# Encoder layer on one core: the split activations and the weight tiles moved to multiples of 2 KB in the SBUF partition

## The chip, the cores and the metric

The kernel runs on one core of one Trainium2 chip. The metric is device time in microseconds, from one launch; lower is better. The matrix engine is called TensorE or PE, its weight loads PEld, the vector engine VectorE or DVE, the scalar engine ScalarE or ACT, the general engine GpSimd or POOL, the engine that issues most DMAs SyncE or SP. SBUF is the on-chip memory with 128 partitions; an address below is a byte offset in a partition, the same for all 128.

## The reference

One encoder layer over 256 positions of width 2048, in float32:

```python
h = rmsnorm(x, norm1_gain)
proj = h @ w_in                       # 2048 x 6144: q, k, v of both head groups
# 4 differential heads: (softmax1 - lam * softmax2) V; 8 dilated-window heads, 3 patterns each
x = x + concat([o_d, o_l]) @ w_out    # 2048 x 2048
h2 = rmsnorm(x, norm2_gain)
g, u = split(h2 @ w_gate_up)          # 2048 x 11264
g = depthwise_conv(g, conv_w, conv_b) # width 3 over positions
x = x + (silu(g) * u) @ w_down        # 5632 x 2048
return rmsnorm(x, final_gain)
```

## The kernel before

Nearly all of the work is in four large matrix products. To keep float32 accuracy on a faster format, every operand is split in two float32r parts, hi (the rounded value) and lo (the remainder), by `split` (L118): ACT copies the value into hi (L121, or L124 with a gain), DVE subtracts hi from the value and writes lo (L122, or L125). A product is then three matmuls that add in PSUM: hi by hi, hi by lo, lo by hi.

The weights come as 196 tiles of 1 MB (`raw`, L80, three buffers). Each is used as two units of 1024 columns; `split_unit` (L198) makes `whi` and `wlo` of a unit (L200 and L201, four buffers each), three units ahead of the matmuls. `products` (L212) issues a unit's matmuls by `mm` (L209), so all of them carry line L210. There are two forms, and every matmul is preceded by a load of its stationary operand:

- Form A, 12 matmuls to a unit: a 128x128 block of the activations is stationary (512 bytes in a partition), 512 columns of weights are moving (2048 bytes). The stages are v (32 units, activations `hT`), o (32 units, `mT`) and d (88 units, `aT`).
- Form B, 24 matmuls to a unit: a 128x128 block of weights is stationary, 256 columns of activations are moving (1024 bytes). The stages are qk (64 units, `hT`) and gate/up (176 units, `h2T`, which has the memory of `hT`).

The stages run in the order v, qk, o, gate/up, d. Post-processing (attention scores, transposes, evacuations) is hung on slots after the units; in qk and o it puts short bursts of other matmuls between units, in gate/up and d none after the first few units.

SBUF is given out by pools. The pool `keep` (L53) comes first, then `stg` (L54: raw, whi, wlo), then `att` (L59) or, after attention, `mlp`. In a pool, tags lie one after the other in the order in which the program first asks for them, each rounded up to 32 bytes. `hT` is asked for at L128, after `sm`, `tl`, `ident`, `ones` and `mhalf`:

```python
mhalf = keep.tile([128, 2], F32, name="mhalf")                 # L115
hT = keep.tile([128, KT, 2, S], F32R, name="hT", tag="hT")     # L128
hi = stg.tile([128, 1024], F32R, name="whi", tag="whi")        # L200
```

What follows in `keep` sets where `stg` begins, and so where everything later begins. The functions that the change touches:

Of the kernel before, what the change touches and what calls it, by code (L numbers as in the profile page):

```python
# [9 lines left out]
F32 = mybir.dt.float32  # L10
F32R = mybir.dt.float32r
# [5 lines left out]
S = 256  # L17
D = 2048
KT = D // 128
# [30 lines left out]
def encoder_layer(ctx, tc, xT_d, x_d, w_d, sm_d, tab_d, fg_d, id_d, oh_d, lnc_d, out_d):  # L50
    nc = tc.nc
    PSUM = bass.MemoryType.PSUM
    keep = ctx.enter_context(tc.tile_pool(name="keep", bufs=1))  # L53
# [13 lines left out]
    nc.vector.memset(warm, 0.0)  # L67
    sm = keep.tile([128, N_SM], F32, name="sm")
    nc.gpsimd.dma_start(sm, sm_d)
    xT = att.tile([128, KT, S], F32, name="xT", tag="mT", bufs=1)  # L70
    tl = keep.tile([128, 1], F32, name="tl")
    nc.scalar.activation(tl, warm[:, :1], AF.Copy)
# [39 lines left out]

    ones = keep.tile([128, 128], F32, name="ones")
    nc.gpsimd.memset(ones, 1.0)
    mhalf = keep.tile([128, 2], F32, name="mhalf")  # L115
    nc.gpsimd.memset(mhalf, -0.5)

    def split(hi, lo, src, gain=None):  # L118
# [6 lines left out]
            nc.vector.scalar_tensor_tensor(lo, src, gain, hi.bitcast(F32),  # L125
                                           op0=ALU.mult, op1=ALU.subtract)

    hT = keep.tile([128, KT, 2, S], F32R, name="hT", tag="hT")  # L128

    def split_x(kt):  # L130
        split(hT[:, kt, 0], hT[:, kt, 1], xT[:, kt], sm[:, C_G1 + kt:C_G1 + kt + 1])
# [649 lines left out]
```

## Time and profile before

| what | value |
|---|---|
| median of 3 runs | 1146.08 us (1145.84 to 1146.66) |
| time of the profiled execution | 1146.24 us |
| its span, first to last instruction | 1144.5 us |
| PE busy | 1132.1 us, 99% of the span |
| PEld busy | 1054.2 us, 92% |
| DVE busy | 677.3 us, 59% |
| ACT busy | 548.4 us, 48% |
| mean granted TensorE clock | 0.995 |

The profiled execution spends 1.7 us outside its span. A matmul's duration in the trace reaches past the start of the next one, since matmuls are pipelined. What a matmul costs is therefore its pitch: the time from its start to the next one's start, read as the length of a piece of the chain divided by the matmuls in it.

### The profile page before, as it was taken

The numbers are of one execution on the slowest core, as the hardware profiler recorded it, in microseconds if no ns is written. First come the engines' busy times: TensorE is split into PE (matmuls) and PEld (weight loads), VectorE is DVE, ScalarE is ACT, GpSimd is POOL, SyncE is SP. The second block draws the span as 40 slices with busy tenths as digits, with TensorE's granted clock in tenths as the row PEclk, the third lists the DMA queues.
The fourth block names the chain that finished last, engine by engine and source line by source line (L and its number), as shares of the span: only waits on it lengthen the run. The fifth ranks groups of instructions, "written<-read, shape, count | busy, mean of one in ns | idle before, by whom it ended". The sixth has DMA issues, their size and how long they took to land.

```text
span 1144.5 us, 18680 instructions
## 1 busy us (share of the span) xinstructions
PE 1132.1 (99%) x7924; PEld 1054.2 (92%) x7924; DVE 677.3 (59%) x841; ACT 548.4 (48%) x770; POOL 21.9 (2%) x40
## 2 busy tenths in 40 slices
PE   8999999999999999999999999999999999999996
PEld 6879999999988899999999999999999888888885
DVE  6845667756656576666666566656565545454543
ACT  7544456565555554444444454445444434343432
POOL 0000000010000000000000000000000000000000
PEclk9999999999999999999999999999999999999998
DMA  9578545454444555555454545454555655555552
GB/s 330 194 258 319 181 169 183 165 195 165 172 157 163 205 184 185 185 184 194 175 201 171 212 155 219 163 207 160 209 183 186 221 192 206 190 187 194 205 186 74
DMA packets 34092, 219.87 MB, mean 192 GB/s; under 512 B 3904, under 2 KB 4288, under 8 KB 9432
## 3 DMA queue, kind: packets, MB, share of 16 engines
q1 hardware_dynamic: 31536, 211.17, 51.5%
q0 software_dynamic: 1776, 6.69, 1.6%
q8 instruction: 62, 1.02, 0.3%
q10 hardware_dynamic: 696, 0.81, 0.2%
q14 instruction: 22, 0.18, 0.0%
HBM read 216.54 MB, written 5.27 MB: 194 GB/s over the span
## 4 chain that ended last, share of the span: by engine, by line
PE 98%; DMA 0%; issue 0%; ACT 0%; DVE 0%; POOLq 0%; POOL 0%; DVEq 0%
PE acc L210 90%; PE at L210 7%; PE at L387 0%; DMA sm<-sm 0%; PE at L518 0%; PE at L452 0%; ACT jk L630 0%; POOLq L777 0%; PE at L248 0%; POOL r L636 0%; PE at L150 0%; DVEq L777 0%; ACT hT L124 0%; DVE x L642 0%; DVE x L628 0%
## 5 line engine op out<-in xcount | busy, mean ns | idle before, releaser
L122 DVE TENSOR_TENSOR wlo<-raw,whi 128x1024 fp32r<-128x1024 f32 (+1 forms) x400 | 475.4, 1201 | 283.3 <-ACT whi L121 283.2
L121 ACT ACTIVATE whi<-raw 128x1024 fp32r<-128x1024 f32 (+1 forms) x400 | 408.9, 1036 | 287.6 <-PE acc L210 213.5
L210 PE MATMUL acc<-h2T,whi 128*128 128x256 f32 x2816 | 360.7, 281 | 0.0
L210 PEld LDWEIGHTS acc<-h2T,whi 128*128 128x128 f32 x2816 | 344.1, 189 | 0.1
L210 PE MATMUL acc<-h2T,wlo 128*128 128x256 f32 x1408 | 194.5, 281 | 0.0
L210 PEld LDWEIGHTS acc<-h2T,wlo 128*128 128x128 f32 x1408 | 178.7, 189 | 0.0
L210 PE MATMUL acc<-whi,aT 128*128 128x512 f32 x528 | 162.8, 389 | 0.0
L210 PE MATMUL acc<-hT,whi 128*128 128x256 f32 x1024 | 128.6, 278 | 0.0
L210 PEld LDWEIGHTS acc<-hT,whi 128*128 128x128 f32 x1024 | 121.7, 188 | 0.1
L210 PEld LDWEIGHTS acc<-whi,aT 128*128 128x128 f32 x528 | 99.1, 188 | 20.7
L210 PE MATMUL acc<-wlo,aT 128*128 128x512 f32 x264 | 102.7, 389 | 0.0
L210 PE MATMUL acc<-whi,hT 128*128 128x512 f32 x256 | 82.1, 399 | 2.0 <-ACT hT L124 2.0
L210 PE MATMUL acc<-whi,mT 128*128 128x512 f32 x256 | 82.7, 395 | 0.0
L210 PE MATMUL acc<-hT,wlo 128*128 128x256 f32 x512 | 68.7, 276 | 0.0
L210 PEld LDWEIGHTS acc<-hT,wlo 128*128 128x128 f32 x512 | 62.9, 188 | 0.0
L210 PEld LDWEIGHTS acc<-whi,hT 128*128 128x128 f32 x256 | 48.8, 191 | 14.3 <-ACT hT L124 2.7
L572 ACT ACTIVATE y<-gs,sm 128x256 f32<-128x256 f32 x44 | 24.1, 595 | 75.3 <-DVE gs L564 75.3
L210 PEld LDWEIGHTS acc<-wlo,aT 128*128 128x128 f32 x264 | 49.5, 188 | 10.1
L210 PEld LDWEIGHTS acc<-whi,mT 128*128 128x128 f32 x256 | 48.1, 188 | 9.7
L210 PE MATMUL at<-whi,aT 128*128 128x512 f32 x176 | 54.4, 389 | 0.0
L210 PE MATMUL acc<-wlo,hT 128*128 128x512 f32 x128 | 50.7, 396 | 0.0
L210 PE MATMUL acc<-wlo,mT 128*128 128x512 f32 x128 | 49.9, 390 | 0.0
(120 smaller groups left out, 617.3 us busy)
## 6 DMA issues: line engine op xcount, KB each, us to landing
raw<-w SPq DMA_DIRECT2D x191, 1024.0 KB, 4.9
raw<-w SPq DMA_DIRECT2D x8, 512.0 KB, 7.6
Z<-Td POOLq DMA_DIRECT2D x1, 3072.0 KB, 20.6
Xb<-Z POOLq DMA_DIRECT2D x12, 192.0 KB, 3.2
x<-x SPq DMA_DIRECT2D x4, 512.0 KB, 12.4
xT<-xT SPq DMA_DIRECT2D x7, 256.0 KB, 6.9
raw<-w SPq DMA_DIRECT2D x4, 256.0 KB, 5.3
fg<-fg POOLq DMA_DIRECT2D x1, 1024.0 KB, 5.0
```

The lines of the kernel that those rows point to most:

```text
L121: nc.scalar.activation(hi, src, AF.Copy)
L122: nc.vector.tensor_sub(lo, src, hi.bitcast(F32))
L210: nc.tensor.matmul(out, lhsT, rhs, start=start, stop=stop)
L572: nc.scalar.activation(y[:, c], gs[:, 1:S + 1], AF.Identity, bias=sm[:, C_CB + f:C_CB + f + 1], scale=w[1])
```

## The change

Two edits. `hT` is asked for right after `sm`, ahead of `tl`, `ident`, `ones` and `mhalf`. And the tile of `mhalf` has 34 columns instead of 2, of which the first two are used as before; the other 128 bytes are filling.

```diff
     sm = keep.tile([128, N_SM], F32, name="sm")
     nc.gpsimd.dma_start(sm, sm_d)
+
+    hT = keep.tile([128, KT, 2, S], F32R, name="hT", tag="hT")
     xT = att.tile([128, KT, S], F32, name="xT", tag="mT", bufs=1)
...
-    mhalf = keep.tile([128, 2], F32, name="mhalf")
+    mhalf = keep.tile([128, 34], F32, name="mhalf")[:, :2]
     nc.gpsimd.memset(mhalf, -0.5)
...
-    hT = keep.tile([128, KT, 2, S], F32R, name="hT", tag="hT")
```

On every engine the instructions stand in the same order with the same operands, shapes and waits; only addresses differ. The places that the declarations give, in bytes from a partition's start and as the remainder by 2048 (the whole hi or lo of one row block of activations is 1024 bytes, one buffer of `whi` or `wlo` 4096 bytes, so all blocks and buffers of a tile share the remainders below, up to multiples of 512):

| tile | before | remainder | after | remainder |
|---|---|---|---|---|
| hT, h2T | 19520 | 1088 | 18432 | 0 |
| ident | 18464 | 32 | 51232 | 32 |
| ones | 18976 | 544 | 51744 | 544 |
| x | 52384 | 1184 | 52512 | 1312 |
| raw, first buffer | 71552 | 1920 | 71680 | 0 |
| whi, first buffer | 96128 | 1920 | 96256 | 0 |
| wlo, first buffer | 112512 | 1920 | 112640 | 0 |
| mT, aT | 128896 | 1920 | 129024 | 0 |
| V0 | 176064 | 1984 | 176192 | 64 |
| qks | 199168 | 512 | 199296 | 640 |
| eT | 207648 | 800 | 207776 | 928 |

Everything behind `mhalf` moves up by 128 bytes. `hT` alone moves by another amount, 1088 bytes down: before it began 64 bytes past a multiple of 128, and now at a multiple of 2048. All of `raw`, `whi`, `wlo`, `mT` and `aT` began 128 bytes before a multiple of 2048.

## Rows read from the trace of the kernel before

**Rows 1.** The page: span, busy time by engine, granted clock in 40 slices.
```profile
span 1144.5 us, 18680 instructions
PE 1132.1 (99%) x7924; PEld 1054.2 (92%) x7924; DVE 677.3 (59%) x841; ACT 548.4 (48%) x770; POOL 21.9 (2%) x40
PEclk9999999999999999999999999999999999999998
```

**Rows 2.** The page: the chain that ended last, shares of the span by line.
```profile
PE acc L210 90%; PE at L210 7%; PE at L387 0%; DMA sm<-sm 0%; PE at L518 0%; PE at L452 0%; ACT jk L630 0%; POOLq L777 0%; PE at L248 0%; POOL r L636 0%; PE at L150 0%; DVEq L777 0%; ACT hT L124 0%; DVE x L642 0%; DVE x L628 0%
```

**Rows 3.** Waits of PE, whole span: us in total, times, longest.
```profile
PE acc L210 <- ACT hT L124: 2.0, 1, 2.0
PE at L106 <- DVE warm L67: 1.2, 1, 1.2
```

**Rows 4.** The page: form B matmuls by group, count, busy us and mean ns.
```profile
L210 PE MATMUL acc<-h2T,whi 128*128 128x256 f32 x2816 | 360.7, 281 | 0.0
L210 PE MATMUL acc<-h2T,wlo 128*128 128x256 f32 x1408 | 194.5, 281 | 0.0
...
L210 PE MATMUL acc<-hT,wlo 128*128 128x256 f32 x512 | 68.7, 276 | 0.0
```

**Rows 5.** Chain, one long piece of gate/up, then one of d: start us, us, what.
```profile
419.91 450.15 PE acc L210 x3822
...
909.79 160.25 PE acc L210 x707
```

**Rows 6.** Chain in v: a long undisturbed piece, then two after breaks.
```profile
12.89 28.15 PE acc L210 x123
...
42.11 11.09 PE acc L210 x48
53.63 11.00 PE acc L210 x48
```

**Rows 7.** Chain in qk: undisturbed piece.
```profile
171.39 6.69 PE acc L210 x59
```

**Rows 8.** Chain in qk, in order, around two bursts of transposes (L452, L387).
```profile
163.66 0.44 PE at L452 x4
164.09 2.83 PE acc L210 x24
166.93 0.71 PE at L210 x6
167.64 2.74 PE acc L210 x24
170.37 0.44 PE at L387 x4
170.81 8.18 PE acc L210 x72
```

**Rows 9.** Chain in o and the start of gate/up, around transposes.
```profile
360.29 2.77 PE acc L210 x12
363.06 0.44 PE at L518 x4
363.50 16.37 PE acc L210 x72
...
399.99 0.87 PE at L518 x8
400.87 8.48 PE acc L210 x72
```

**Rows 10.** Windows in v and gate/up: PE, PEld, DVE, ACT, POOL busy, PEclk, DMA share, GB/s.
```profile
70.00:100.00 30.00, 30.00 (x138) 24.82 (x137) 12.69 (x11) 12.71 (x14) 2.86 (x5) 1.00 0.92 358
...
420.00:870.00 450.00, 450.00 (x3823) 450.00 (x3822) 278.19 (x319) 205.10 (x240) 0.00 (x0) 1.00 0.52 187
```

**Rows 11.** Weight DMAs: KB each, median us to landing.
```profile
raw<-w SPq DMA_DIRECT2D x191, 1024.0 KB, 4.9
```

## The prediction

> **What bounds the kernel now.** [...] The waits then tell whether anybody feeds PE too late: it waits for other engines 3.2 us in the whole span [rows 3]. So neither DMA nor ACT nor DVE sets the time. The only thing left that can move it by much is how fast PE itself takes one matmul after the other, its pitch.
>
> The long pieces of the chain give that pitch, and here the reader is to see something odd. In gate/up it is 450.15 us / 3822 = 117.78 ns; in d 160.25 / 707 = 226.66 ns [rows 5]. In v, the same form and shape as d, it is 28.15 / 123 = 228.86 ns [rows 6]. In an undisturbed piece of qk, the same form, shape and even the same addresses as gate/up, it is 6.69 / 59 = 113.39 ns [rows 7]. [...] These pieces hold no wait, and the pitch stays the same over hundreds of microseconds while ACT and DVE work in bursts beside it: it is a gait of PE with its two streams, the stationary load and the moving operand.
>
> What sets the two slow stages apart is `hT`: v and gate/up read it, and it begins 64 bytes past a multiple of 128. The stages o and d read only tiles that begin at multiples of 128 (`mT`, `aT`, `whi`, `wlo`). After a break, o starts slowly too, 2.77 / 12 = 230.8 ns, but settles: 16.37 / 72 = 227.4 ns with that start included [rows 9]. In v it never settles: 231.0 and 229.2 ns over the 48 matmuls after two breaks [rows 6].
>
> **The change part by part.** No instruction is added, removed or moved, and no wait; the memset of `mhalf` still covers two columns. What changes is addresses, and the terms are these.
>
> 1. Gate/up: 2,816 + 1,408 = 4,224 matmuls [rows 4]. If with `hT` at a multiple of 128 they take the gait of the undisturbed piece of qk, each saves 117.78 − 113.39 = 4.39 ns, in all 18.5 us. Bounds: nothing saved, 0, if the gait has nothing to do with the start; a loss where both operands start alike, for which the nearest row is the burst of score products on `qks`, whose two operands begin at multiples of 512: 0.71 / 6 = 118.3 ns [rows 8], so 4,224 × 0.5 = 2 us more; and on the gaining side one pair of load and matmul cannot well be shorter than the pairs of 128 columns in a transpose, 0.44 / 4 = 110 ns [rows 8], so 4,224 × 7.8 = 33 us. I take 18.5, because the qk row is the same instruction on the same tiles.
> 2. v: 32 units of 12 are 384 matmuls; at the pitch of d each saves 228.86 − 226.66 = 2.2 ns, together 0.8 us. [...]
> 3. qk: 64 × 24 = 1,536 matmuls, mostly in the good gait. After the bursts of four transposes at L452 a unit runs at 2.83 / 24 = 117.9 ns against 2.74 / 24 = 114.2 later [rows 8], and there are only a few such bursts: 0.4 us at most. Bounds: 0.4 gained, or 1,536 × (118.3 − 114) = 6.6 us lost if the rate of the `qks` burst became the rule.
> 4. o and d, 384 + 1,056 matmuls: relative to each other their operands keep their places, both move by 128 bytes. I take 0; bounds in the rivals.
> 5. ACT, DVE, DMA: the tiles they read and write move too. I take 0. In the gate/up window ACT is busy 205 of 450 us and DVE 278 [rows 10], and both wait for PE rather than the reverse; DVE would have to grow by half to show. A faster PE asks for weights 4% faster, 187 GB/s becoming 195; in v the same queues move 358 GB/s [rows 10], and a tile lands in 4.9 us [rows 11] where two units take 5.4 us even at the good gait, with three buffers. Without that cover a late tile would cost what it is late, at most a few tenths each.
>
> Sum: 18.5 + 0.8 + 0.4 = 19.7 us off the profiled execution's 1146.24, that is 1126.5; its 1146.24 is 0.16 above the median, so I say 1126.4.
>
> [...]
>
> **The rivals.**
>
> No change, 1146 (1144.5 to 1147.8). The two gaits of form B occur at the same addresses: in qk 24 matmuls at 117.9 ns follow a burst of transposes, and after the next burst the rate is 113.6 (8.18 / 72) [rows 8]. So the gait may hang on the state in which PE leaves a break, and gate/up, which no break disturbs after its first units, keeps the slow one that it fell into at 8.48 / 72 = 117.8 ns [rows 9]. For it: the address alone cannot explain qk. Against it: v never settles and o always does, at equal form and shape. Chance 27%.
>
> Slower, about 1155 (1149 to 1161). Now all large operands begin at the same remainder of 2048, so stationary load and moving operand could meet in the same part of memory on each step. The one place where a pair with such a relation is seen is the `qks` burst, at 118.3 ns, worse than any steady row [rows 8]. If that became the rule of form B, gate/up would lose 2 and qk 6.6 us, 1155; if form A kept the 230.8 ns of its starts [rows 9], o and d would add 1,440 × 4.1 = 6 us. It decides from a form B pitch above 117.8. Against it: o and d already have operands that begin at the same remainder and are the best of form A; and six matmuls after a break need not be a steady state. Chance 14%.
>
> [...] Chance 14%.
>
> **How the numbers follow.** Forecast 1126.4 (1122 to 1130), chance 42%; the three rivals 27, 14 and 14; 3% for a gain in one stage only, 1131 to 1143. Faster by over 0.2% (2.3 us, about what a measurement of this kernel can tell): 42 + 14 + 2 = 58%. Within it: 27 less 1 at its edge, 26%. Slower: 14 and the rest, 16%. The range reaches from 1108, which takes in the weaker half of the third rival, over the forecast and no change to 1150, the near edge of the slower case: about 8 in 10. The forecast's own range stands above.
>
> **What would show it.** In the changed profile the chain's long piece in gate/up should have about 3,970 matmuls in 450 us, a pitch of 113.4, and the mean of `acc<-h2T,whi` should drop from 281 to the 276 ns that the group on `hT` has [rows 4]; v should read 226.7; o and d should stay at 226.7, and PE should still wait for nobody. Gate/up at 117.8 with v at 226.7 would mean that the start matters for form A alone and that form B goes by its entry. Both unchanged: the no-change rival. [...] A d above 227 or a gate/up above 118: operands that meet. The forecast is wrong altogether if PE begins to wait for `whi`, or if the clock is no longer granted in full.

## The result: slower, 1164.5 us

| | before | after |
|---|---|---|
| median of 3 runs | 1146.08 us (1145.84 to 1146.66) | 1164.48 us (1163.74 to 1164.95) |
| profiled execution | 1146.24 us | 1164.95 us |
| its span | 1144.5 us | 1163.2 us |

The ratio after to before is 1.0159, with a 95% interval of 1.0136 to 1.0182. The forecast was 1126.4 us with a range up to 1150, so the time lies outside the range and on the other side. Lines after L69 have a number one or two higher than before; the matmuls are now L211.

### The profile page after: what moved, and what is told of

The parts are those of the page before. It is cut to its first block, busy times and chain, and to the rows that moved or that the text cites. A ratio compares the mean times of both kernels' runs of the same rounds, so it can differ in the third digit from the quotient of the medians.

```text
span 1163.2 us, 18680 instructions
## 1 busy us (share of the span) xinstructions
PE 1151.0 (99%) x7924; PEld 1073.8 (92%) x7924; DVE 677.8 (58%) x841; ACT 550.4 (47%) x770; POOL 22.0 (2%) x40
## 4 chain that ended last, share of the span: by engine, by line
PE 98%; DMA 0%; issue 0%; ACT 0%; DVE 0%; POOLq 0%; POOL 0%; DVEq 0%
PE acc L211 90%; PE at L211 7%; PE at L388 0%; DMA sm<-sm 0%; PE at L453 0%; PE at L519 0%; ACT jk L631 0%; POOLq L778 0%; PE at L249 0%; POOL r L637 0%; PE at L151 0%; DVEq L778 0%; ACT hT L126 0%; DVE x L643 0%; DVE x L629 0%
## 5 line engine op out<-in xcount | busy, mean ns | idle before, releaser
L211 PE MATMUL acc<-h2T,whi 128*128 128x256 f32 x2816 | 366.9, 283 | 0.0
L211 PEld LDWEIGHTS acc<-h2T,whi 128*128 128x128 f32 x2816 | 350.7, 192 | 0.1
L211 PE MATMUL acc<-h2T,wlo 128*128 128x256 f32 x1408 | 197.6, 283 | 0.0
L211 PEld LDWEIGHTS acc<-h2T,wlo 128*128 128x128 f32 x1408 | 181.6, 192 | 0.0
L211 PE MATMUL acc<-whi,aT 128*128 128x512 f32 x528 | 162.8, 389 | 0.0
L211 PE MATMUL acc<-hT,whi 128*128 128x256 f32 x1024 | 134.5, 284 | 0.0
L211 PEld LDWEIGHTS acc<-hT,whi 128*128 128x128 f32 x1024 | 127.2, 192 | 0.1
L211 PEld LDWEIGHTS acc<-whi,aT 128*128 128x128 f32 x528 | 99.1, 188 | 20.7
L211 PE MATMUL acc<-wlo,aT 128*128 128x512 f32 x264 | 102.7, 389 | 0.0
L211 PE MATMUL acc<-whi,hT 128*128 128x512 f32 x256 | 82.3, 400 | 1.8 <-ACT hT L126 1.8
L211 PE MATMUL acc<-whi,mT 128*128 128x512 f32 x256 | 82.7, 395 | 0.0
L211 PE MATMUL acc<-hT,wlo 128*128 128x256 f32 x512 | 71.9, 283 | 0.0
L211 PEld LDWEIGHTS acc<-hT,wlo 128*128 128x128 f32 x512 | 66.0, 192 | 0.0
L211 PEld LDWEIGHTS acc<-whi,hT 128*128 128x128 f32 x256 | 49.4, 193 | 14.0 <-ACT hT L126 2.7
L211 PEld LDWEIGHTS acc<-wlo,aT 128*128 128x128 f32 x264 | 49.6, 188 | 10.1
L211 PEld LDWEIGHTS acc<-whi,mT 128*128 128x128 f32 x256 | 48.1, 188 | 9.7
L211 PE MATMUL at<-whi,aT 128*128 128x512 f32 x176 | 54.4, 389 | 0.0
L211 PE MATMUL acc<-wlo,hT 128*128 128x512 f32 x128 | 51.0, 398 | 0.0
L123 ACT ACTIVATE aT<-a 128x512 fp32r<-128x512 f32 x22 | 13.9, 631 | 76.1 <-DVE a L589 76.1
```

Source lines behind the costliest of these rows:

```text
L123: nc.scalar.activation(hi, src, AF.Copy)
L211: nc.tensor.matmul(out, lhsT, rhs, start=start, stop=stop)
```

## The profile after

The head of the page, against [rows 1]: the span, busy time of each engine, and the granted clock in 40 slices.

```profile
span 1163.2 us, 18680 instructions
...
PE 1151.0 (99%) x7924; PEld 1073.8 (92%) x7924; DVE 677.8 (58%) x841; ACT 550.4 (47%) x770; POOL 22.0 (2%) x40
...
PEclk9999999999999999999999999999999999999998
```

Only PE and its loads grew: PE's busy time went from 1132.1 to 1151.0 us, while DVE and ACT stay within 2 us of theirs. The granted clock is 0.997 on the mean, 0.995 before. The waits of PE, against [rows 3], say that nobody feeds it later:

```profile
PE acc L211 <- ACT hT L126: 1.8, 1, 1.8
PE at L108 <- DVE warm L67: 1.2, 1, 1.2
```

So the 18.7 us that the span grew by have to be pitch. The pieces of the chain that answer to [rows 5 to 8], in order of time (start us, us, what): v, then qk around two bursts of transposes, then gate/up, then d.

```profile
12.87 28.34 PE acc L211 x125
...
167.20 0.44 PE at L453 x4
167.64 2.88 PE acc L211 x24
170.51 0.72 PE at L211 x6
171.23 2.88 PE acc L211 x24
174.11 0.44 PE at L388 x4
174.55 8.62 PE acc L211 x72
...
429.98 450.12 PE acc L211 x3751
...
929.87 160.25 PE acc L211 x707
```

Divide each by its count. Gate/up is 450.12 / 3751 = 120.0 ns, where it was 117.78 [rows 5] and where I forecast 113.4. In qk every piece is now at 120.0 or 119.7 ns, also those that ran at 114 before [rows 8]: the bursts no longer change anything. Stage v is at 226.7 ns instead of 228.86 [rows 6], as forecast, and d stays at 226.66.

The matmuls by tile say which stage pays (columns: least, median and greatest ns of one, first and last start, shape): qk, gate/up and d.

```profile
L211 PE MATMUL acc<-hT,whi x1024: 278/283/365, 99.0 to 309.9; 128*128 128x256 f32 x171
...
L211 PE MATMUL acc<-h2T,whi x2816: 278/283/467, 406.3 to 913.4; 128*128 128x256 f32 x188
...
L211 PE MATMUL acc<-whi,aT x528: 389/389/396, 914.5 to 1093.8; 128*128 128x512 f32 x176
```

The same view of the kernel before has 98.8 to 300.6, 397.0 to 894.7 and 895.8 to 1075.1. So qk takes 210.9 instead of 201.8 us, 9.1 more; gate/up 507.1 instead of 497.7, 9.4 more (4,224 x 2.22 ns = 9.4); d 179.3 in both; and v begins at 6.6 in both and hands over 0.2 later. The sum, 18.7 us, is the whole difference of the spans. The gain in v is there in each matmul and does not come through as time: the first 144 matmuls took 35.76 us instead of 34.89, and the loss lies ahead of 12.87 us. There PE takes its first matmuls at half pace, 5.12 us for 12 of them from 7.39 us on, 427 ns each; in the kernel before this pace ends at 11.1 instead of 12.7 us. The clock granted in the kernel before is 0.50 from 8.5 to 10.5 us; the profile of the changed kernel says 1.00 there at the same slow pace, so that the clock is the cause in both is not shown. The length of this start does not go by the distances: the kernel with the filling alone, below, has those of the kernel before, and the long start too (36.1 us for the 144 matmuls, at 28.40 / 124 = 229.0 ns each behind the start).

## The experiments

Below, "distance" is the start of the moving operand less the start of the stationary one, modulo 256 bytes; blocks and columns step by multiples of 256, so a stage has one distance. The change moved hT and the weights from 1088 and 1920 (modulo 2048) to 0 and 0. In form B that turns distance 192 into 0; in form A of stage v, where the activations are stationary, 64 into 0; in o and d it was 0 and stays 0.

**hT early, without the filling.** The changed kernel with one line undone: hT begins at 0, the weights at 1920 as before. Form B then has distance 128, v too.

```diff
-    mhalf = keep.tile([128, 34], F32, name="mhalf")[:, :2]
+    mhalf = keep.tile([128, 2], F32, name="mhalf")
```

> Only hT moves, to remainder 0 of 2048; whi, wlo, mT and aT stay at remainder 1920. Theory R (only how the starts of the two operands of a matmul lie to each other in steps of 128 bytes counts; 0 apart is the bad case of form B): gate/up and qk at 120.0 ns, v at 226.7 ns, time 1164 as with the whole change. Rival S (operands must begin at the same remainder of 2048, or of 512, to meet): 128 bytes apart they do not, form B at 117.8 ns or less, time 1127 to 1147. Rival F (the move of the weight tiles by the filling is what costs): 1146 or less.

It took 1158.98 us, 1.0111 of before (1.0094 to 1.0128). The chain of this kernel, a piece of v, then one of gate/up:

```profile
12.86 28.23 PE acc L211 x121
...
429.98 450.10 PE acc L211 x3793
```

That is 233.3 and 118.67 ns, and none of the expectations has these numbers. The miss has a reason that the scan below shows: the distances repeat with a period of 256 bytes, not 128 as theory R said (32 matmuls of form A take 7.29 us at 0 and at 256, and 7.44 at 128). What falls is the premise of my forecast that a start of the activations at a multiple of 128 is enough: hT is at 0 here, and both stages are slower than before.

**The filling alone.** The kernel before with 128 bytes more ahead of hT. Both operands move by 128 (hT 1216, weights 0), so every distance between them is as before.

```diff
-    mhalf = keep.tile([128, 2], F32, name="mhalf")
+    mhalf = keep.tile([128, 34], F32, name="mhalf")[:, :2]
```

> Only the filling: hT, whi, wlo, mT and aT all move up by 128 bytes together, so hT is at remainder 1216 (64 past a multiple of 128) and the weights at 0. Theory R: nothing in the relation of the operands changes, gate/up 117.8 ns, qk mostly 113.4, v 228.9, time 1146 within 1. Rival F: gate/up at 120 ns and 1155 to 1164. Rival X (a moving operand pays for each multiple of 1024 or 2048 that it crosses): d and o faster than 226.7 ns, time below 1140.

It took 1127.86 us, 0.984 of before (0.9825 to 0.9854). Only rival X had a time below 1140, and by a faster d and o; d stayed at 226.7 ns, so no expectation had this gain. The chain of this kernel from the start of gate/up, then a long piece:

```profile
400.67 0.88 PE at L518 x8
401.55 8.48 PE acc L210 x72
410.03 0.43 PE at L150 x2
410.46 39.57 PE acc L210 x349
...
429.97 440.07 PE acc L210 x3883
```

The reader is to see the place where it turns: 8.48 / 72 = 117.8 ns ahead of the two small matmuls of L150, and 39.57 / 349 = 113.4 behind them. In the kernel before the first of these rows is the same [rows 9] and the pitch stays at 117.8 behind L150. From there on the good gait holds to the end of the stage, 440.07 / 3883 = 113.33 ns. L150 multiplies two tiles of which one lies ahead of the filling and one behind; that this is why the break ends differently is argued, not shown. It fits that a filling of 256 bytes, below, ends this break as the kernel before does. So at one distance two gaits are stable, and a break of 0.43 us picks one for 4,000 matmuls.

**Distance 64 in form B.** The changed kernel with hT moved up by 64 bytes, the weights still at 0.

```diff
+    keep.tile([128, 16], F32, name="gap")
     hT = keep.tile([128, KT, 2, S], F32R, name="hT", tag="hT")
...
-    mhalf = keep.tile([128, 34], F32, name="mhalf")[:, :2]
+    mhalf = keep.tile([128, 18], F32, name="mhalf")[:, :2]
```

> The changed kernel with hT 64 bytes further (remainder 64 of 2048), weights at remainder 0 as in the change. Theory R: form B comes back to the pitches of before (117.8 or 113.4 ns), v to 228.9, time 1127 to 1147. Rival S would expect the same; rival F (weights at 0 cost) 1164.

1153.37 us, 1.0065 of before (1.005 to 1.008), outside the 1127 to 1147 that theory R gave. Gate/up is at 117.78 ns, as before, and v, now at distance 192, at 28.23 / 121 = 233.3 instead of the 228.9 expected. The rest of the loss is qk, which runs at 117.8 ns throughout (8.01 / 68 in the longest piece read): 1,536 matmuls by up to 4.4 ns are at most 6.7 us, and v's 384 by 4.4 are 1.7.

```profile
13.00 28.23 PE acc L212 x121
...
429.89 450.15 PE acc L212 x3822
```

**Distances by themselves.** A kernel of bursts alone, with the layer left out: 64 form B matmuls (n256) or 32 form A matmuls (n512), with the moving operand m and the stationary one s bytes past a multiple of 2048, four transposes between bursts in the first pass (a), none in the second (b). It ran once, and no other engine works during the bursts: DVE, ACT and POOL are busy for 0.00 us from 80 to 124 and from 355 to 520 us.

```python
nc.tensor.matmul(p[:, c, :n], sta[:, st + lhs * 128:st + (lhs + 1) * 128],
                 mov[:, m + rhs:m + rhs + n], start=..., stop=...)
```

> No layer: bursts of matmuls alone, 64 of form B (256 moving columns) and 32 of form A (512), with the start of the moving operand (m) or of the stationary one (s) set to 0 to 448 bytes past a multiple of 2048; once after four transposes (a), once in the reverse order without a break (b). The output is not the layer's. Theory R: form B 120 ns at m0s0, m128s0, m256s0, m384s0 and where m equals s; 113 to 118 at m64s0, m192s0, m320s0; form A 226.7 at multiples of 128 and 228.9 at 64. Rival S: 120 only at m0s0 and where m equals s, or at steps of 512. If the pitch follows m and s differently when they are equal, the start itself counts, not the relation.

The chain of this kernel, some of its bursts (start us, us, burst):

```profile
24.16 7.67 PE n256m0s0a L81 x64
...
56.30 7.54 PE n256m64s0a L81 x64
...
80.49 7.29 PE n256m112s0a L81 x64
...
104.28 7.54 PE n256m192s0a L81 x64
...
160.20 7.28 PE n256m0s64a L81 x64
...
200.12 7.67 PE n256m64s64a L81 x64
...
208.22 7.29 PE n512m0s0a L81 x32
...
439.88 7.27 PE n256m192s0b L81 x64
```

Three things are read off. First, equal starts cost 7.67 / 64 = 119.8 ns wherever they are (0 and 0, 64 and 64), so it is the distance and not the place. Second, m192s0 takes 7.54 in one pass and 7.27 in the other, 117.8 and 113.6 ns: two gaits at one distance, without any other engine at work. Distance 64 has the same pair: m64s0 took 7.54 in both passes, and m320s0, whose distance is 64 too, 7.26 and 7.54. Third, distance 0, among the slowest of form B, is the best of form A: 7.29 / 32 = 227.8 ns with the start included, against 7.33 to 7.50 us at the others. Theory R's steps of 128 fall here: form A takes 7.44 us at m128s0 (232.5 ns) and 7.29 at m256s0. Two limits belong to this. Distance 0 is not alone at the slow end, as m96s0 takes 7.68 us in both passes. And that the distance alone sets the pitch is not shown for every one: at distance 240, m0s16 takes 120.0 and 118.3 ns here, and a moving start of 240 takes 117.3 ns after four different breaks in the second burst kernel below.

**Both moved by 256.** The kernel before with 256 bytes more ahead of hT: no distance changes, and the places of all operands do.

```diff
-    mhalf = keep.tile([128, 2], F32, name="mhalf")
+    mhalf = keep.tile([128, 66], F32, name="mhalf")[:, :2]
```

> Filling of 256 bytes instead of 128, hT created where it was: all large tiles move up by 256 bytes against the kernel before, by 128 against the kernel with the filling alone. The starts of hT and of the weights stay 192 bytes apart in steps of 256. Theory G (the distance in steps of 256 allows form B two gaits, 113.3 and 117.8 ns, and the last break before gate/up picks one): either 1127 or 1146, nothing between, with the change of gait at a break and never inside a run. Rival A (the remainder by 256 of the start itself sets the pitch: the weights at 128 slow, at 0 fast): gate/up 117.8 ns from the first to the last unit, 1146.

1146.32 us, 1.0003 of before (0.9993 to 1.0012), with gate/up at 117.78 ns:

```profile
429.93 450.15 PE acc L210 x3822
```

Both sides allowed this time, so the run did not tell them apart.

**Breaks in gate/up.** The kernel before, with nine short bursts put between units of gate/up: 1, 2, 3, 4 and 8 transposes, 1, 2 and 6 matmuls on h2T, and 2 transposes again. No address changes.

```diff
+    KICKS = (("t", 1), ("t", 2), ("t", 3), ("t", 4), ("t", 8), ("m", 1), ("m", 2), ("m", 6), ("t", 2))
...
+    for i, how in enumerate(KICKS):
+        at_slot(end_slot["g", 3 + 2 * i] + 1, kick, *how)
```

> The kernel before, addresses kept, with nine short bursts put between units of gate/up (one at every second pair from the fourth on): 1, 2, 3, 4, 8 transposes, then 1, 2 and 6 matmuls of 256 columns on h2T alone, then 2 transposes; their results are not used. Theory G: some bursts throw form B from 117.8 to 113.3 ns (and perhaps others back), each piece between two bursts runs at one of the two pitches to its end, and the time is below 1146 by 4.4 ns times the matmuls in the good gait, though the bursts cost some 5 us themselves. Rival A: 117.8 ns in every piece, about 1151.

One run, 1142.26 us. The chain of this kernel through gate/up (L599 are the transposes):

```profile
409.56 70.67 PE acc L210 x600
480.23 0.11 PE at L599
480.34 43.55 PE acc L210 x384
523.89 0.22 PE at L599 x2
524.11 43.55 PE acc L210 x384
567.67 0.33 PE at L599 x3
568.00 45.23 PE acc L210 x384
613.23 0.44 PE at L599 x4
613.66 43.54 PE acc L210 x384
```

384 matmuls take 43.55 us (113.4 ns) behind 1, 2 or 4 transposes and 45.23 (117.8 ns) behind 3; behind 8 transposes and behind the three bursts on h2T it was 45.23 too, and behind the last 2 transposes the pitch was 113.3 ns again (46.13 / 407). A break can turn the gait either way, and it lasts until the next break. That settles that at distance 192 the break ahead of a piece decides, and that nothing in the addresses of gate/up forces the 117.8 ns of the kernel before.

**Distance 112.** The kernel before with hT early and both hT and h2T 112 bytes into their tile, the weights at a multiple of 2048.

```diff
+    def h_tile(name):
+        t = keep.tile([128, KT * 2 * S + 32], F32R, name=name, tag="hT")
+        return t[:, 28:28 + KT * 2 * S].rearrange("p (k h s) -> p k h s", k=KT, h=2)
```

> hT and h2T begin 112 bytes past a multiple of 2048 and the weights at a multiple of 2048. In the scan the distance 112 gave form B 113.3 ns in both passes, while 64, 192 and 320 gave 113.3 or 117.8. Theory G: gate/up and qk at 113.3 ns from a few matmuls after each break, without luck; v, whose distance is then 144 in steps of 256, at 232 to 235 ns, 2 us worse than before; together 1127 to 1129. If 112 too has a second gait, 1146 or so. Rival A (the start itself): weights at 0 as in the kernel with the filling alone, so 1128 as well, but a different pitch in the scan.

1129.7 us, 0.9859 of before (0.9843 to 0.9875), 0.7 above the range expected. The chain of this kernel, v, the start of gate/up and a long piece of it:

```profile
12.91 28.23 PE acc L215 x121
...
402.75 8.22 PE acc L215 x72
...
429.89 440.19 PE acc L215 x3884
```

Gate/up has 114.2 ns from its first units on, where other kernels begin at 117.8, and 113.33 in its long piece (440.19 / 3884). Stage v pays with 233.3 ns, since its distance is now 144.

**How long a gait lasts.** Bursts alone again, the layer left out, run once: each distance from 0 to 240 in steps of 16 four times with 48 matmuls, and 64, 112, 192 and 208 twice with 240.

> Matmul bursts alone, the output is not the layer's: form B with the moving start 0 to 240 bytes (steps of 16) past a multiple of 2048 and the stationary start at one; each of 48 matmuls after four transposes (a), after two (b), after six matmuls of 512 columns (c) and after the burst before (d); then 240 matmuls at 64, 112, 192 and 208 after four transposes (e) and after one (f); then form A at 112, 144, 176, 208. Theory G: a distance has a fixed set of pitches; at 0 only 120, at 112 only 113.3, at 64 and 192 113.3 or 117.8 by the break; and a gait once taken lasts through 240 matmuls. Against it would be a pitch that drifts within a burst, or differs between a, b, c and d at every distance.

The chain of this kernel, distance 192 twice in short bursts, then 112 and 192 in long ones:

```profile
319.69 5.46 PE m192a L81 x48
325.36 5.66 PE m192b L81 x48
...
475.44 27.28 PE m112e L81 x240
...
530.49 28.27 PE m192e L81 x240
```

At 192 the gait is 113.8 or 117.9 ns by the break, and the slow one is still there after 240 matmuls (117.8). At 112 all six bursts are fast: 5.44 to 5.50 us for 48, 27.22 and 27.28 for 240. The number of transposes alone does not pick the gait: at 192 four of them lead into the fast one in m192a and into the slow one in m192e, and two, which brought the fast one in gate/up, lead into the slow one in m192b.

**A version that takes the good gaits.** hT at 192 (form A at distance 64 in v, form B at 192 in qk, where breaks are many) and h2T at 112 (gate/up), the weights 256 bytes past a multiple of 2048.

```diff
+    def h_tile(name):
+        t = keep.tile([128, KT * 2 * S + 64], F32R, name=name, tag="hT")
+        f = 48 if name == "hT" else 28
+        return t[:, f:f + KT * 2 * S].rearrange("p (k h s) -> p k h s", k=KT, h=2)
```

> hT 192 bytes and h2T 112 bytes past a multiple of 256, the weights at a multiple of 256. Theory G: v (distance 64 in steps of 256) at 229 ns instead of the 233.6 with hT at 112, 1.7 us less; qk at 113.3 ns but for a few units in the other gait; gate/up at 113.3 ns whatever the breaks; 1126.5 to 1128.5, at or below the 1127.9 of the kernel with the filling alone. If the gait could be lost at 112 too: up to 1146.

1127.67 us, 0.9841 of before (0.9827 to 0.9854). The chain of this kernel, a piece of v, then one of gate/up:

```profile
12.84 28.39 PE acc L216 x124
...
429.98 440.07 PE acc L216 x3883
```

That is 229.0 ns in v and 113.33 in gate/up. It beats both kernels of this case, by 18.4 and by 36.8 us of their medians. No break led to the slow gait at distance 112, in gate/up of the two kernels that have it there or in the bursts: every piece read has 113.3 to 114.6 ns.

**One break alone.** The kernel before with two transposes after the fifth unit of gate/up (the expectation says the sixth), and no address changed.

```diff
+    def kick():
+        p = at_tile()
+        for c in (0, 128):
+            nc.tensor.transpose(out=p[:, c:c + 128], in_=xs[0][:, 0, c:c + 128], identity=ident)
+
+    at_slot(e_o + 5, kick)
```

> The kernel before with all its addresses, and one burst of two transposes (result unused) after the sixth unit of gate/up. Theory G: gate/up leaves it at 113.3 ns and keeps that to its end, some 4,000 matmuls by 4.4 ns less a burst of 0.3 us: 1128 to 1129. Rival A (the start itself sets the pitch): 117.8 ns to the end, 1146.

1128.37 us, 0.9844 of before (0.9831 to 0.9857). The chain of this kernel, v, the start of gate/up and a long piece of it:

```profile
12.68 28.47 PE acc L210 x122
...
409.74 0.43 PE at L150 x2
410.17 2.83 PE acc L210 x24
413.00 0.22 PE at L548 x2
413.23 61.78 PE acc L210 x545
...
429.90 440.19 PE acc L210 x3884
```

Ahead of the two transposes the pitch is 2.83 / 24 = 117.9, behind them 61.78 / 545 = 113.4 ns. They cost 0.22 us and bring 18. Beside it v shows that form A has two gaits as well: 28.47 / 122 = 233.4 ns in this piece, at the addresses at which the kernel before had 228.86 [rows 6]; later in v it is back at 229.0.

## Why the prediction was wrong

What bounds the kernel was read rightly: PE's pitch and nothing else. In the changed kernel and in the experiments the difference lies in the pitch of v, qk and gate/up; PE waits 3.0 us in all in the changed kernel and 2.9 in the mixed version.

**The step that failed is term 1**, "if with hT at a multiple of 128 they take the gait of the undisturbed piece of qk", worth 18.5 us. Gate/up took 120.0 ns, a loss of 9.4 us instead, where the bound on the losing side was 2. The argument was that the two slow stages read hT, which began 64 past a multiple of 128, and that o and d, which read only tiles at multiples of 128, were at the best pitch. That is evidence on form A, and it was carried over to form B. The runs show that the start of one operand is not what matters: distance 0, which o and d have, is the best of form A and among the slowest of form B (226.66 in d and 120.0 in gate/up, in one kernel). The row that I took as the goal, 113.39 ns in qk [rows 7], had been run at the old addresses; it was the good one of two gaits of distance 192. I had written that down as the point for no change, and still used the row as if it belonged to the new addresses.

**Term 3** had the other sign for the same reason. I took 0.4 us gained and named 6.6 lost as the bound; qk lost 9.1, since at 120.0 ns its good pieces went too. The bound was too near, because the 118.3 ns of the `qks` burst [rows 8] was taken as the price of equal starts. The same six matmuls take 0.72 us in the changed kernel, 120 ns. One unit in the last digit of such a short piece, 0.01 of 0.71 us, is 1.4%, and that is the whole difference; a row of six matmuls could not carry that price.

**Term 2** was right in size, 2.2 ns for each matmul of v, and did not show in the stage's length, as the first 144 matmuls, with a longer stretch at half pace, took 0.9 us more. That the size came out is luck, as its reason was that of term 1: v came to 226.7 ns with its distance at 0; in the kernel with hT alone moved, where hT begins at a multiple of 128 too, it was 233.3. **Terms 4 and 5** held: o and d kept their pitch, and no engine or transfer became late (a weight tile lands in 4.8 us, 4.9 before [rows 11]).

**The rivals.** The slower one, at 14%, had the condition, equal starts of load and moving operand, and the sign; that the two then meet in one part of memory is not shown. Its price was too low (118.3 instead of 120.0 ns, so 1155 instead of 1164), and its doubt about o and d was unfounded. "No change" was right that entry picks the gait of gate/up, which two transposes prove (1146.2 to 1128.4 at equal addresses), and wrong that addresses then cannot matter: they decide which gaits there are. The third, faster than the forecast and the reason why the range began at 1108, charged a moving operand for each multiple of 1024 that it crosses. No run shows such a price: in the changed kernel, where the moving operands begin at remainder 0 and cross one multiple fewer, d kept 226.66 ns and gate/up went from 117.78 to 120.0.

No other engine is needed for the difference: with DVE, ACT and POOL idle in the bursts, the pitch of one instruction goes from 113.6 ns at distance 192 (m192s0, second pass) to 119.8 at distance 0.

The forecast's time was within reach by another edit: the filling, which is one half of this change, gives 1127.86 by itself, and the mixed version 1127.67. That the filling comes so near to the forecast is luck, as its gain hangs on how one break ends. The loss needs the other half, the move of hT: alone it gives 1158.98, and with the filling, which puts hT at the weights' remainder, 1164.48.

## What to carry to other kernels

When PE is the bound, divide long pieces of the chain by their counts and compare stages with the same form only; the best pitch of another form said nothing here (at distance 0 d has 226.66 ns, its best, and gate/up 120.0). Ask for the distance of the two operands modulo 256 bytes before aligning either of them: aligning both alike was among the slowest choices for 256 moving columns (120.0 ns, against 113.3 at distance 112). If the same instruction at the same addresses shows two pitches, try short breaks: two transposes turned gate/up twice here, but left a burst at the same distance in the slow gait, so measure what a break does. Where the stage is long, choose a distance at which only the fast gait was seen.

## What the runs showed of the hardware

Pitch of float32r matmuls with a load for each, by distance, at a granted clock of 0.995 to 0.998 on the mean of each profiled run; two values joined by "or" are two gaits. Bursts that include their start are marked *:

| distance | 256 moving columns | 512 moving columns |
|---|---|---|
| 0 | 120.0 ns | 226.7 ns |
| 64 | 113.4* or 117.8 | 228.9 or 233.4 |
| 112 | 113.3 | 231.3* |
| 128 | 118.6 to 120.0 | 233.3 |
| 192 | 113.3 or 117.8 | 233.3 |

At 192 both gaits were seen through thousands of matmuls; at 64 the fast one only in bursts of 48 and 64. Other distances show more values in the bursts, as 117.3 to 120.0 ns at 160. For comparison, one float32 product of 256 columns (L150, kernel before) is two matmuls in the chain and takes 0.43 us. Not expected were the period of 256, that a gait lasts through thousands of matmuls (3,822 at 117.78 ns, 3,883 at 113.33), and that in one kernel three transposes led into the slow one (117.8 ns) and two or four into the fast one (113.4). What stays open is why: whether and where the two reads meet, why 256 columns dislike what 512 like, and what in a break picks the gait. That the mixed version is better than the filling alone isn't shown either (1127.67 and 1127.86); the mixed version only leaves less to a break.
